# Two-layer hybrid decoder trunk: FFN parts of 4, 4 and 3 blocks, a first FFN block in one pass, and whole 512-column pieces

## The chip, the cores and the metric

The kernel runs on one core of one Trainium2 chip. The metric is the device time of one execution in microseconds (us), the median of the runs.

## The reference

The input x has 256 tokens of 2048 float32 values. Each of two layers computes, in float32:

```
h = RMSNorm(x);  x = x + mixer(h)            # mLSTM, forgetting attention, gated DeltaNet; ends in y @ w_out
h = RMSNorm(x);  x = x + (silu(h @ w_gate) * (h @ w_up)) @ w_down      # w_gate, w_up: 2048 x 5632
```

A last RMSNorm follows. The change touches the product with w_out at the end of the mixer, the whole FFN, and the norms' sums of squares.

## The kernel before

**Weights.** They lie in HBM in the order of use as units of 128 x 1024 float32 (512 KB). `unit` loads one into a `raw` buffer (3 buffers, SP's queue) and splits it: ScalarE writes the rounded `whi` (L140), VectorE the rest `wlo` (L141); there are 4 buffers of each. Activations are split into hi and lo in the same way. Each product is three matmuls, hi·whi, hi·wlo and lo·whi, into one PSUM bank. `block_b` does that for two token tiles of 128 (t = 0, 1), a weight piece of w columns and kts tiles of the contraction.

**PSUM.** There are eight banks: four of tag `d` (`dps`), two of `mg`, one each of `m0` and `m1` (`mps`).

**Order.** Tile's scheduler puts the instructions into the engines' queues. It follows the program's order but may take a later instruction ahead of one that is not ready by its own simulated times; each engine then runs its queue strictly in order. `tc.issue_after` holds instructions behind a given one. Semaphores come from the tiles.

**wo and the next norm.** The mixer's output product (L780 to 803) writes 512 columns of x at a time, the last 512 as two halves of 256. After each piece, `add_x` adds it into `xall` (VectorE), and `Norm.piece` transposes those columns (tile xT, by TensorE), splits them into the next operand `hs`, and sums squares. `Norm.scale` turns the sums into rstd (a power, by POOL) and into `rb`, rstd along the free axis, by two small matmuls (rbp) and a copy.

**FFN.** `ffn` (L810) takes the 5632 hidden columns in 11 blocks of 512, and the blocks in parts (`FF_PARTS`, 2, 2, 2, 2, 2, 1). After a part's blocks, its share of the product with w_down (`dn`) is added to x, in pieces of 512 columns; in the last part the last 512 come as two halves.

- The first block (`slow`) multiplies the unnormalised `hs`: all 16 k-tiles for gate (pg), then all 16 for up (pu). rstd is applied afterwards. Then `normalise(rb)` rescales `hs` in place for the other blocks, per k-tile: POOL adds hi and lo (yn, L841), VectorE multiplies by rb (L842), ScalarE rounds (L843), VectorE subtracts (L844); POOL forms the difference of the two token tiles (dt, L856; three sums st for the pairs), ScalarE and VectorE split that into `sd` (L829, L830).
- The other ten blocks (`fast`) use a 7-product scheme on two pairs of k-tiles (`quad`, k = 3 and 11) and a four-product form elsewhere (`plain`), in seven PSUM accumulators. Products 1, 6 and 7 end at k = 11 and are taken into `xs`, `ys`; products 2 to 5 end with the block, and VectorE and ScalarE form `ga`.
- Then the block's `ga` is transposed (tile hT, 8 transposes in two groups, bank `m0`) and split into `hid`, down's operand.

**The end.** In layer 1 the last half piece of down runs one token tile after the other (`block_b_halves`), and `Final.last` scales and stores each.

Of the kernel before, what the change touches and what calls it, by code (L numbers as in the profile page):

```python
# [23 lines left out]
KT = D // P  # L24
DFF = 5632
FT = DFF // P
FF_PARTS = (2, 2, 2, 2, 2, 1)
PAIRS = (3, 11)
HM, HF, HG = 4, 8, 4
EPS = 1e-6  # L30
# [29 lines left out]
def tile_trunk(ctx: ExitStack, tc: tile.TileContext, x: bass.AP, wu: bass.AP, prm: bass.AP,  # L60
# [170 lines left out]
        pool.tensor_tensor(out=r, in0=r, in1=mhalf[:, :cols], op=ALU.pow)  # L231
        return r

    PIECES = (slice(0, 512), slice(512, 1024), slice(1024, 1536), slice(1536, 1792), slice(1792, 2048))

    def square_sum(ssq, j, both=False):
        c = PIECES[j]
        w = c.stop - c.start
        for t in range(2):
            if both and t:  # L240
                junk = sp.tile([P, 512], BF16, tag="junkv", name="junkv", bufs=1)
                dve.scalar_tensor_tensor(out=junk[:, :w], in0=xall[:, t, c], scalar=1.0, in1=xall[:, t, c],
                                         op0=MUL, op1=MUL, accum_out=ssq[:, t, j:j + 1])
            else:
                junk = sp.tile([P, 512], BF16, tag="junk", name="junk", bufs=1)
                act.activation(out=junk[:, :w], in_=xall[:, t, c], func=AF.Square, accum_out=ssq[:, t, j:j + 1])
# [6 lines left out]
    class Norm:  # L253


        def __init__(self, l, off):
            self.l, self.off, self.hs = l, off, []
            self.ssq = small("ssq", [2, 5])

        def pair(self, k):  # L260
            ps = mps("xT")
# [8 lines left out]
                self.hs.append((hl[:, :S], hl[:, S:], hl))  # L270

        def piece(self, j):
            for k in range(PIECES[j].start // P, PIECES[j].stop // P, 2):
                self.pair(k)
            square_sum(self.ssq, j)

        def scale(self, first=False):
            if first:
                for j in range(5):
# [74 lines left out]
    def mixer(l, norm, nxt):  # L354
# [435 lines left out]
        for n in range(2):  # L790
            wout(n, groups[n], late, False, True)
            add_x(n, groups[n])
            nxt.piece(n)
        pst = [dps("wo") for t in range(2)]
        wout(2, pst, early + late, True, True)
        add_x(2, pst)
        nxt.piece(2)
        for c in range(2):
            pst = [dps("wo") for t in range(2)]
            for i, k in enumerate((0, 12, 4, 8)):  # L800
                block_b(l, "out", 1536 + c * S, pst, ys[k:k + 4], k, 4, i == 0, i == 3, S)
            add_x(3, pst, c * S, S)
            nxt.piece(3 + c)

    def add_x(n, pst, c=0, w=512, ts=(0, 1)):
        for t in ts:
# [3 lines left out]
    def ffn(l, norm, nxt):  # L810
# [19 lines left out]
            dve.tensor_tensor(out=e[:, 1], in0=v, in1=f32(e[:, 0]), op=SUB)  # L830
            return e[:, 0], e[:, 1]

        def normalise(rb):

            free = [sd[i][:, j] for i in range(5) for j in range(4)]
            free = [v.rearrange("p (h x) -> p h x", h=2) if len(v.shape) == 2 else v for v in free]
            y = [None, None]
            for k in range(KT):
                hi, lo, hl = hs[k]
                y[k % 2] = yk = sp.tile([P, S], F32, tag="ac", name="yn", bufs=2)  # L840
                pool.tensor_tensor(out=yk, in0=f32(hi), in1=f32(lo), op=ADD)  # L841
                dve.tensor_tensor(out=yk, in0=yk, in1=rb, op=MUL)  # L842
                act.activation(out=hi, in_=yk, func=AF.Copy)  # L843
                dve.tensor_tensor(out=lo, in0=yk, in1=f32(hi), op=SUB)  # L844
                if k - 1 in PAIRS:
                    y0 = y[1 - k % 2]
                    st = sp.tile([P, 384], F32, tag="pt", name="st", bufs=2)
                    s1, s2, s4 = (st[:, i * P:(i + 1) * P] for i in range(3))
                    pool.tensor_tensor(out=s1, in0=y0[:, P:], in1=yk[:, P:], op=ADD)
                    pool.tensor_tensor(out=s2, in0=s1, in1=y0[:, :P], op=SUB)  # L850
                    pool.tensor_tensor(out=s4, in0=yk[:, :P], in1=s2, op=SUB)
                    for n, v in (("s1", s1), ("s2", s2), ("s4", s4)):
                        ops[n, k - 1] = hilo(free.pop(), v)
                else:
                    v = sp.tile([P, S], F32, tag="tz", name="dt", bufs=2)[:, :P]
                    pool.tensor_tensor(out=v, in0=yk[:, :P], in1=yk[:, P:], op=SUB)  # L856
                    ops["d", k] = hilo(free.pop(), v)

        def quad(c, k):

# [31 lines left out]

        def fast(c, first):

            ps = {3: dps("p3")}
            for i in ((1, 6, 7) if first else (2, 4, 5)):
                ps[i] = dps(f"p{i}")
            for i, tag in zip((2, 4, 5) if first else (6, 7, 1), ("mg", "mg", "m1")):
                ps[i] = mps(f"p{i}", tag)
            seen = set()  # L900
            for k in range(KT):
                if k - 1 in PAIRS:
                    continue
                for i, (ahi, alo), (whi, wlo) in quad(c, k) if k in PAIRS else plain(c, k):
                    end = k == KT - 1 or (i in (1, 6, 7) and k == PAIRS[-1])
                    pe.matmul(ps[i], ahi, whi, start=i not in seen, stop=False)
                    pe.matmul(ps[i], ahi, wlo, start=False, stop=False)
                    pe.matmul(ps[i], alo, whi, start=False, stop=end)
                    seen.add(i)
                if k == PAIRS[-1]:  # L910
                    act.copy(out=xs[:, 0], in_=ps[1])
                    dve.tensor_tensor(out=xs[:, 1], in0=ps[6], in1=xs[:, 0], op=ADD)
                    dve.tensor_tensor(out=ys[:, 0], in0=ps[7], in1=xs[:, 1], op=ADD)
            for t, i, v in ((0, 2, xs[:, 0]), (1, 4, ys[:, 0])):
                dve.tensor_tensor(out=ga[:, t], in0=ps[i], in1=v, op=ADD)
                act.activation(out=ga[:, t], in_=ga[:, t], func=AF.Silu)
            dve.tensor_tensor(out=ys[:, 1], in0=ps[5], in1=xs[:, 1], op=ADD)
            dve.tensor_tensor(out=ys[:, 0], in0=ps[5], in1=ys[:, 0], op=ADD)
            dve.tensor_tensor(out=ys[:, 1], in0=ps[3], in1=ys[:, 1], op=ADD)
            for t in range(2):  # L920
                dve.tensor_tensor(out=ga[:, t], in0=ga[:, t], in1=ys[:, 1 - t], op=MUL)

        def slow(c):
            pg = [dps("pg") for t in range(2)]
            block_b(l, "gate", c, pg, hs, 0, KT, True, True)
            rstd, rb = norm.scale()
            for t in range(2):
                act.activation(out=ga[:, t], in_=pg[t], func=AF.Silu, scale=rstd[:, t:t + 1])
            pu = [dps("pu") for t in range(2)]
            block_b(l, "up", c, pu, hs, 0, KT, True, True)  # L930
            for t in range(2):
                dve.scalar_tensor_tensor(out=ga[:, t], in0=pu[t], scalar=rstd[:, t:t + 1], in1=ga[:, t],
                                         op0=MUL, op1=MUL)
            normalise(rb)

        for part, blocks in enumerate(FF_PARTS):
            nf = 4 * blocks
            fs = []
            for c in range(f0 * P, (f0 + nf) * P, 512):
                if c == 0:  # L940
                    slow(c)
                else:
                    fast(c, c == 512 or c == f0 * P)
                for q in range(0, 4, 2):
                    ps = mps("hT", "m0")
                    for i in range(2):
                        for t in range(2):
                            pe.transpose(ps[:, i * S + t * P:i * S + (t + 1) * P],
                                         ga[:, t, (q + i) * P:(q + i + 1) * P], ident)
                    hid = g4("hid", [2, 512], F32R, "gy")  # L950
                    act.copy(out=hid[:, 0], in_=ps)  # L951
                    dve.tensor_tensor(out=hid[:, 1], in0=ps, in1=f32(hid[:, 0]), op=SUB)
                    fs += [(hid[:, 0, i * S:(i + 1) * S], hid[:, 1, i * S:(i + 1) * S]) for i in range(2)]
            end = part == len(FF_PARTS) - 1
            for n in range(3 if end else 4):
                pst = [dps("dn") for t in range(2)]
                block_b(l, "down", n * 512, pst, fs, f0, nf, True, True)
                add_x(n, pst)
                if end:
                    nxt.piece(n)  # L960
            if end:
                for c in range(2):
                    pst = [dps("dn") for t in range(2)]
                    if c and l == depth - 1:
                        block_b_halves(l, "down", 1536 + c * S, pst, fs, f0, nf, S)
                        for t in range(2):
                            add_x(3, pst, c * S, S, (t,))
# [90 lines left out]
```

## Time and profile before

| | |
|---|---|
| median of 3 runs | 2416.74 us (2416.14 to 2416.99) |
| profiled execution | 2416.53 us, span 2414.6 us |
| TensorE busy | 2368.0 us, 98% of the span |
| VectorE, ScalarE, POOL busy | 1680.2, 1212.0, 278.3 us |
| mean granted TensorE clock | 0.992 |
| DMA | 435.89 MB, mean 181 GB/s |

Times are from the span's start. A stretch is read by its count of matmuls and the pace of one, since busy time of TensorE has modelled ends. Layer 0's FFN is 467.3 to 1209.6 us, layer 1's 1662.7 to 2405.

### The profile page before, as it was taken

To read this page: it belongs to the slowest core of one execution; us is meant where nothing else is said; L and a number is where in the kernel's file an instruction comes from. 1 tells how busy PE (TensorE), PEld (TensorE's weight loads), DVE (VectorE), ACT (ScalarE), POOL (GpSimd) and SP (SyncE) were. 2 spreads that over 40 slices of the span, in tenths; PEclk is the share of its full clock that TensorE was granted. 3 is DMA by queue.
4 is the path that set the end of the run, shared out by engine and by line. 5 is a ranking of instruction groups with operands and counts; after the bars stand their busy time and mean duration, and the time that the engine had idled before them with its cause. 6 is when DMAs were issued, how large, how long until landed. Compare 5 with 4: busy or idle time off the path is not lost.

```text
span 2414.6 us, 31866 instructions
## 1 busy us (share of the span) xinstructions
PE 2368.0 (98%) x11852; PEld 1995.4 (83%) x11852; DVE 1680.2 (70%) x2366; ACT 1212.0 (50%) x1783; POOL 278.3 (12%) x259
## 2 busy tenths in 40 slices
PE   9999999989999999999899999999999999999997
PEld 8888888867888888888798888888788888888886
DVE  5898655587676768576668976555866767676756
ACT  6754555554444444454466545555544444444443
POOL 0220000050101111010003000000501010111100
PEclk9999999999999999999999999999999999999998
DMA  6555455546565656665455554455465656565663
GB/s 218 167 174 175 138 166 176 176 166 198 175 210 191 200 185 200 191 198 183 151 169 175 175 163 152 155 186 192 148 200 191 201 169 213 192 196 186 203 203 114
DMA packets 120876, 435.89 MB, mean 181 GB/s; under 512 B 13584, under 2 KB 14480, under 8 KB 120720
## 3 DMA queue, kind: packets, MB, share of 16 engines
q1 hardware_dynamic: 120160, 432.70, 55.3%
q8 instruction: 93, 1.52, 0.3%
q10 hardware_dynamic: 560, 1.15, 0.1%
q14 instruction: 63, 0.52, 0.1%
HBM read 431.70 MB, written 2.10 MB: 180 GB/s over the span
## 4 chain that ended last, share of the span: by engine, by line
PE 88%; DVE 4%; issue 2%; ACT 2%; DMA 2%; POOL 1%; POOLq 0%; DVEq 0%; SPq 0%; ACTq 0%
PE p L70 31%; PE dn L70 19%; PE wo L70 7%; PE fq L70 4%; PE fk L70 4%; PE fv L70 4%; PE gkq L70 3%; PE mv L70 2%; DMA raw<-wu 2%; PE mq L70 2%; PE mk L70 2%; PE gvp L70 2%; PE gz L70 2%; PE pg L70 2%; DVE wlo L141 1%
## 5 line engine op out<-in xcount | busy, mean ns | idle before, releaser
L141 DVE TENSOR_TENSOR wlo<-raw,whi 128x1024 fp32r<-128x1024 f32 (+3 forms) x741 | 918.7, 1247 | 473.5 <-ACT whi L140 455.0
L140 ACT ACTIVATE whi<-raw 128x1024 fp32r<-128x1024 f32 (+3 forms) x741 | 775.8, 1053 | 772.2 <-PE dn L70 244.3
L70 PE MATMUL p<-whi,hl 128*128 128x512 f32 x1600 | 546.6, 391 | 1.0 <-ACT whi L140 1.0
L70 PE MATMUL dn<-whi,hid 128*128 128x512 f32 (+1 forms) x1440 | 444.3, 389 | 3.8 <-ACT hid L951 1.3
L70 PEld LDWEIGHTS p<-whi,hl 128*128 128x128 f32 x1600 | 301.3, 188 | 63.5 <-ACT whi L140 1.9
L70 PE MATMUL p<-wlo,hl 128*128 128x512 f32 x800 | 313.2, 392 | 7.1 <-DVE wlo L141 7.1
L70 PEld LDWEIGHTS dn<-whi,hid 128*128 128x128 f32 x1440 | 268.2, 189 | 60.0 <-ACT whi L140 3.0
L70 PE MATMUL dn<-wlo,hid 128*128 128x512 f32 (+1 forms) x720 | 277.2, 389 | 1.3 <-DVE wlo L141 1.3
L70 PE MATMUL p<-whi,sd 128*128 128x512 f32 x560 | 216.3, 391 | 0.0
L70 PEld LDWEIGHTS p<-wlo,hl 128*128 128x128 f32 x800 | 150.5, 188 | 41.0 <-DVE wlo L141 9.8
L874 POOL TENSOR_TENSOR rq<-rq 128x512 f32<-128x512 f32 x40 | 57.4, 1436 | 989.5 <-DVE rq L873 973.7
L70 PE MATMUL wo<-whi,yhl 128*128 128x512 f32 (+1 forms) x640 | 169.5, 351 | 0.0
L70 PEld LDWEIGHTS dn<-wlo,hid 128*128 128x128 f32 x720 | 136.5, 190 | 32.1 <-DVE wlo L141 5.2
L70 PEld LDWEIGHTS wo<-whi,yhl 128*128 128x128 f32 x640 | 112.6, 189 | 14.7
L70 PEld LDWEIGHTS p<-whi,sd 128*128 128x128 f32 x560 | 105.9, 189 | 21.6
L70 PE MATMUL wo<-wlo,yhl 128*128 128x512 f32 (+1 forms) x320 | 111.8, 349 | 0.0
L70 PE MATMUL p<-wlo,sd 128*128 128x512 f32 x280 | 109.8, 392 | 0.0
L878 ACT ACTIVATE th<-rq 128x1024 fp32r<-128x1024 f32 x80 | 84.0, 1050 | 43.8 <-POOL rq L876 27.8
L879 DVE TENSOR_TENSOR tl<-rq,th 128x1024 fp32r<-128x1024 f32 x80 | 99.8, 1248 | 3.5 <-ACT th L878 3.1
L876 POOL TENSOR_TENSOR rq<-rq 128x512 f32<-128x512 f32 x40 | 83.1, 2078 | 120.5 <-DVE rq L875 117.4
L871 DVE TENSOR_TENSOR wlo<-rq,whi 128x1024 fp32r<-128x1024 f32 x40 | 56.1, 1401 | 52.9 <-ACT whi L870 52.8
L870 ACT ACTIVATE whi<-rq 128x1024 fp32r<-128x1024 f32 x40 | 42.4, 1060 | 98.0 <-PE p L70 98.0
(362 smaller groups left out, 3527.2 us busy)
## 6 DMA issues: line engine op xcount, KB each, us to landing
raw<-wu SPq DMA_DIRECT2D x728, 512.0 KB, 4.2
rq<-wu SPq DMA_DIRECT2D x80, 512.0 KB, 4.2
raw<-wu SPq DMA_DIRECT2D x10, 420.0 KB, 3.0
xall<-x SPq DMA_DIRECT2D x3, 512.0 KB, 8.3
fw<-fnw SPq DMA_DIRECT2D x2, 512.0 KB, 6.8
out<-xall ACTq DMA_DIRECT2D x2, 512.0 KB, 3.3
out<-xall SPq DMA_DIRECT2D x2, 512.0 KB, 3.3
xall<-x SPq DMA_DIRECT2D x2, 256.0 KB, 4.4
```

Source lines behind the costliest of these rows:

```text
L70: self.log.append(nc.tensor.matmul(*a, **k).ins)
L140: act.activation(out=whi[:, c], in_=raw[:, c], func=AF.Copy)
L141: dve.tensor_tensor(out=wlo[:, c], in0=raw[:, c], in1=f32(whi[:, c]), op=SUB)
L870: act.activation(out=w1[0], in_=r1, func=AF.Copy)
L871: dve.tensor_tensor(out=w1[1], in0=r1, in1=f32(w1[0]), op=SUB)
L874: pool.tensor_tensor(out=b12, in0=b22, in1=b12, op=SUB)
L876: pool.tensor_tensor(out=b21, in0=b21, in1=b22, op=SUB)
L878: act.activation(out=hi, in_=v, func=AF.Copy)
L879: dve.tensor_tensor(out=lo, in0=v, in1=f32(hi), op=SUB)
```

## The change

The first block reads gate and up columns of one k-tile in one unit, has four accumulators open, and normalises a k-tile behind its matmuls. The transposes of a block's `ga` are kept as `pending` and issued inside the next `fast` block behind k = 5 and k = 7, or inside down's first piece behind its first two groups of four k-tiles. The parts are 4, 4 and 3 blocks. Which products of a block lie in the `d` banks now follows from its distance to the part's end. The last 512 columns of wo, and of down except at the end of layer 1, are one piece; the norms sum squares over four pieces.

```diff
-FF_PARTS = (2, 2, 2, 2, 2, 1)
+FF_PARTS = (4, 4, 3)
...
-    PIECES = (slice(0, 512), slice(512, 1024), slice(1024, 1536), slice(1536, 1792), slice(1792, 2048))
+    QUARTERS = tuple(slice(c, c + 512) for c in range(0, D, 512))
+    PIECES = QUARTERS[:3] + (slice(1536, 1792), slice(1792, 2048))
...
         def piece(self, j):
-            for k in range(PIECES[j].start // P, PIECES[j].stop // P, 2):
+            for k in range(4 * j, 4 * j + 4, 2):
                 self.pair(k)
             square_sum(self.ssq, j)
...
-        pst = [dps("wo") for t in range(2)]
-        wout(2, pst, early + late, True, True)
-        add_x(2, pst)
-        nxt.piece(2)
-        for c in range(2):
+        for n in range(2, 4):
             pst = [dps("wo") for t in range(2)]
-            for i, k in enumerate((0, 12, 4, 8)):
-                block_b(l, "out", 1536 + c * S, pst, ys[k:k + 4], k, 4, i == 0, i == 3, S)
-            add_x(3, pst, c * S, S)
-            nxt.piece(3 + c)
+            wout(n, pst, early + late, True, True)
+            add_x(n, pst)
+            nxt.piece(n)
...
-        def normalise(rb):
+        def normalise(k, rb):
...
-            ps = {3: dps("p3")}
-            for i in ((1, 6, 7) if first else (2, 4, 5)):
-                ps[i] = dps(f"p{i}")
+            ps = {i: dps(f"p{i}") for i in ((1, 6, 7, 3) if first else (2, 4, 5, 3))}
...
+                if k in (5, 7) and pending:
+                    hidden()
...
         def slow(c):
-            pg = [dps("pg") for t in range(2)]
-            block_b(l, "gate", c, pg, hs, 0, KT, True, True)
-            rstd, rb = norm.scale()
+
+            pg, pu = ([dps(n) for t in range(2)] for n in ("pg", "pu"))
+            for k in range(KT):
+                whi, wlo = unit(("s", l, "ug", c, k, 1, 1024))
+                for j, pst in ((1, pg), (0, pu)):
+                    w = slice(j * 512, (j + 1) * 512)
+                    for t in range(2):
+                        ahi, alo = half(k, t)
+                        pe.matmul(pst[t], ahi, whi[:, w], start=(k == 0), stop=False)
+                        pe.matmul(pst[t], ahi, wlo[:, w], start=False, stop=False)
+                        pe.matmul(pst[t], alo, whi[:, w], start=False, stop=(k == KT - 1))
+                if k == 0:
+                    rstd, rb = norm.scale()
+                normalise(k, rb)
...
-            pu = [dps("pu") for t in range(2)]
-            block_b(l, "up", c, pu, hs, 0, KT, True, True)
...
-            normalise(rb)
+
+        pending = []
+
+        def hidden():
+
+            fs, q = pending.pop(0)
+            ps = mps("hT", "m0")
+            with tc.issue_after(pe.log[-1]):
+                for i in range(2):
+                    for t in range(2):
+                        pe.transpose(ps[:, i * S + t * P:i * S + (t + 1) * P],
+                                     ga[:, t, (q + i) * P:(q + i + 1) * P], ident)
+            hid = g4("hid", [2, 512], F32R, "gy")
+            act.copy(out=hid[:, 0], in_=ps)
+            dve.tensor_tensor(out=hid[:, 1], in0=ps, in1=f32(hid[:, 0]), op=SUB)
+            fs += [(hid[:, 0, i * S:(i + 1) * S], hid[:, 1, i * S:(i + 1) * S]) for i in range(2)]
...
-                    fast(c, c == 512 or c == f0 * P)
...
+                    fast(c, (blocks - n) % 2 == 1)
+                pending += [(fs, 0), (fs, 2)]
             end = part == len(FF_PARTS) - 1
+            end = end and l == depth - 1
             for n in range(3 if end else 4):
                 pst = [dps("dn") for t in range(2)]
-                block_b(l, "down", n * 512, pst, fs, f0, nf, True, True)
+                for j in range(0, nf, 4):
+                    block_b(l, "down", n * 512, pst, fs[j:j + 4], f0 + j, 4, j == 0, j == nf - 4)
+                    if n == 0 and j < 8:
+                        hidden()
                 add_x(n, pst)
-                if end:
+                if part == len(FF_PARTS) - 1:
                     nxt.piece(n)
             if end:
                 for c in range(2):
                     pst = [dps("dn") for t in range(2)]
-                    if c and l == depth - 1:
+                    if c:
                         block_b_halves(l, "down", 1536 + c * S, pst, fs, f0, nf, S)
```

## Rows read from the trace of the kernel before

**Rows 1.** The page: busy time, share of the span and instructions of each engine.

```profile
PE 2368.0 (98%) x11852; PEld 1995.4 (83%) x11852; DVE 1680.2 (70%) x2366; ACT 1212.0 (50%) x1783; POOL 278.3 (12%) x259
```

**Rows 2.** The chain of waits, TensorE's pieces: start us, us, what, count.

```profile
447.26 10.80 PE wo L70 x90
...
472.39 0.33 PE xT L73 x3
...
1003.24 51.00 PE p L70 x225
```

**Rows 3.** Windows: stretch, us, then busy us (instructions) of each engine, granted clock, DMA.

```profile
467.30:1209.60 742.30, 727.05 (x3247) 596.69 (x3246) 520.47 (x572) 353.38 (x425) 100.11 (x77) 0.99 0.58 187
1662.70:2405.00 742.30, 727.54 (x3230) 596.31 (x3229) 520.06 (x573) 347.83 (x415) 100.99 (x75) 0.99 0.57 185
...
517.00:538.00 21.00, 14.41 (x54) 9.48 (x54) 19.95 (x30) 11.90 (x23) 15.57 (x15) 0.92 0.30 100
561.00:575.00 14.00, 12.82 (x57) 10.00 (x56) 11.62 (x14) 6.34 (x7) 0.00 (x0) 1.00 0.72 246
...
1174.00:1188.00 14.00, 7.49 (x27) 5.53 (x26) 8.06 (x11) 3.68 (x6) 0.00 (x0) 0.76 0.38 114
1712.50:1733.20 20.70, 15.15 (x54) 10.05 (x52) 19.65 (x30) 11.90 (x23) 15.56 (x15) 0.84 0.31 100
...
2370.00:2385.00 15.00, 8.49 (x28) 6.36 (x28) 8.48 (x12) 4.15 (x6) 0.00 (x0) 0.66 0.40 127
```

**Rows 4.** The same windows, instructions of tile xT alone.

```profile
467.30:1209.60 742.30, 3.15 (x20) 2.44 (x20) 4.15 (x9) 4.09 (x9) 0.99 0.58 187
1662.70:2405.00 742.30, 0.76 (x4) 0.52 (x4) 0.96 (x2) 0.93 (x2) 0.99 0.57 185
```

**Rows 5.** Timeline of TensorE at the last FFN part of layer 0.

```profile
1175.29 0.39 PE L70 MATMUL p<-whi,sd 128*128 128x512 f32 x1
1181.52 1.09 PE L73 MATMUL hT<-ident,ga 128*128 128x128 f32 x4 [5.84 <-DVE ga L921]
```

**Rows 6.** Timeline of VectorE in the same stretch.

```profile
1178.35 1.22 DVE L141 TENSOR_TENSOR wlo<-raw,whi 128x1024 fp32r<-128x1024 f32 x1
```

**Rows 7.** Timeline of TensorE in the block after the first.

```profile
528.01 0.65 PE L70 MATMUL p<-wlo,hl 128*128 128x512 f32 x1 [2.92 <-DVE wlo L141]
```

**Rows 8.** Groups by line, 489 to 545 us: busy us, mean ns | idle.

```profile
L141 DVE TENSOR_TENSOR wlo<-raw,whi 128x1024 fp32r<-128x1024 f32 x13 | 17.3, 1333 | 5.3 <-ACT whi L140 5.3
...
L856 POOL TENSOR_TENSOR dt<-yn 128x128 f32<-128x128 f32 x14 | 13.7, 980 | 30.8 <-DVE yn L842 28.5 <-ACT whi L870 1.4 <-ACT sd L829 0.9
L140 ACT ACTIVATE whi<-raw 128x1024 fp32r<-128x1024 f32 x13 | 13.6, 1048 | 1.6 <-PE p L70 1.5
...
L841 POOL TENSOR_TENSOR yn<-hl 128x256 f32<-128x256 f32 x14 | 12.0, 869 | 5.1 <-DVE hl L844 5.1
L842 DVE TENSOR_TENSOR yn<-yn,rb 128x256 f32<-128x256 f32 x16 | 9.7, 616 | 1.1 <-POOL yn L841 1.1
...
L830 DVE TENSOR_TENSOR sd<-dt,sd 128x128 fp32r<-128x128 f32 x14 | 7.4, 543 | 0.1
L844 DVE TENSOR_TENSOR hl<-yn,hl 128x256 fp32r<-128x256 f32 x16 | 7.3, 463 | 0.5 <-ACT hl L843 0.5
```

**Rows 9.** Two lines over the whole span: ns least/median/greatest, first and last start.

```profile
L842 DVE TENSOR_TENSOR yn<-yn,rb x32: 410/416/1489, 493.8 to 1737.2; 128x256 f32<-128x256 f32 x32
...
L830 DVE TENSOR_TENSOR sd<-dt,sd x28: 277/528/830, 496.9 to 1738.5; 128x128 fp32r<-128x128 f32 x28
```

**Rows 10.** Timelines of TensorE and POOL where the first FFN block begins.

```profile
467.32 0.40 PE L70 MATMUL pg<-whi,hl 128*128 128x512 f32 x1
...
470.19 0.71 POOL L231 TENSOR_TENSOR rstd<-rstd,mhalf 128x2 f32<-128x2 f32 x1 [45.94 <-DVE rstd L230]
```

**Rows 11.** The end: the chain of waits, and VectorE's timeline.

```profile
2406.32 1.38 issue
...
2407.51 0.15 DVE L230 TENSOR_SCALAR frstd<-fs 128x1 f32<-128x1 f32 x1
```

More of the change, by code (lines that the diff above doesn't have):

```diff
@@ L232, in rstd_of @@
         return r
-    PIECES = (slice(0, 512), slice(512, 1024), slice(1024, 1536), slice(1536, 1792), slice(1792, 2048))
+    QUARTERS = tuple(slice(c, c + 512) for c in range(0, D, 512))
+    PIECES = QUARTERS[:3] + (slice(1536, 1792), slice(1792, 2048))
     def square_sum(ssq, j, both=False):
-        c = PIECES[j]
+        c = (QUARTERS if ssq.shape[-1] == 4 else PIECES)[j]
         w = c.stop - c.start
@@ L257, in __init__ @@
             self.l, self.off, self.hs = l, off, []
-            self.ssq = small("ssq", [2, 5])
+            self.ssq = small("ssq", [2, 4])
         def pair(self, k):
@@ L278, in scale @@
             if first:
-                for j in range(5):
+                for j in range(4):
                     square_sum(self.ssq, j, True)
@@ L831, in hilo @@
             return e[:, 0], e[:, 1]
-        def normalise(rb):
[L835 to L857, printed above, removed]
@@ new lines, in ffn @@
+        free = [sd[i][:, j] for i in range(5) for j in range(4)]
+        yn = [None, None]
+        def normalise(k, rb):
+            hi, lo, hl = hs[k]
+            yn[k % 2] = yk = sp.tile([P, S], F32, tag="ac", name="yn", bufs=2)
+            pool.tensor_tensor(out=yk, in0=f32(hi), in1=f32(lo), op=ADD)
+            dve.tensor_tensor(out=yk, in0=yk, in1=rb, op=MUL)
+            act.activation(out=hi, in_=yk, func=AF.Copy)
+            dve.tensor_tensor(out=lo, in0=yk, in1=f32(hi), op=SUB)
+            if k - 1 in PAIRS:
+                y0 = yn[1 - k % 2]
+                st = sp.tile([P, 384], F32, tag="pt", name="st", bufs=2)
+                s1, s2, s4 = (st[:, i * P:(i + 1) * P] for i in range(3))
+                pool.tensor_tensor(out=s1, in0=y0[:, P:], in1=yk[:, P:], op=ADD)
+                pool.tensor_tensor(out=s2, in0=s1, in1=y0[:, :P], op=SUB)
+                pool.tensor_tensor(out=s4, in0=yk[:, :P], in1=s2, op=SUB)
+                for n, v in (("s1", s1), ("s2", s2), ("s4", s4)):
+                    ops[n, k - 1] = hilo(free.pop(), v)
+            else:
+                v = sp.tile([P, S], F32, tag="tz", name="dt", bufs=2)[:, :P]
+                pool.tensor_tensor(out=v, in0=yk[:, :P], in1=yk[:, P:], op=SUB)
+                ops["d", k] = hilo(free.pop(), v)
@@ L938, in ffn @@
             fs = []
-            for c in range(f0 * P, (f0 + nf) * P, 512):
+            for n in range(blocks):
+                c = (f0 + 4 * n) * P
                 if c == 0:
@@ L942, in ffn @@
                 else:
-                    fast(c, c == 512 or c == f0 * P)
[L944 to L953, printed above, removed]
+                    fast(c, (blocks - n) % 2 == 1)
+                pending += [(fs, 0), (fs, 2)]
             end = part == len(FF_PARTS) - 1
+            end = end and l == depth - 1
             for n in range(3 if end else 4):
                 pst = [dps("dn") for t in range(2)]
-                block_b(l, "down", n * 512, pst, fs, f0, nf, True, True)
+                for j in range(0, nf, 4):
+                    block_b(l, "down", n * 512, pst, fs[j:j + 4], f0 + j, 4, j == 0, j == nf - 4)
+                    if n == 0 and j < 8:
+                        hidden()
                 add_x(n, pst)
-                if end:
+                if part == len(FF_PARTS) - 1:
                     nxt.piece(n)
```

## The prediction

> **What bounds the kernel now.** I read the page's engine line first: TensorE alone is near its span [rows 1]. That share is made of modelled matmul ends, so it does not say whether TensorE keeps its pace. The pace comes from the chain of waits: 225 matmuls of 512 columns in 51.00 us are 0.227 us each, 90 of 256 columns in 10.80 us are 0.120, three transposes in 0.33 us are 0.11 [rows 2]. Below, "loss" is TensorE's elapsed time less its instructions at these paces.
>
> The windows over the two FFN stages come next: 742.3 us each [rows 3]. By the code, one holds 3084 matmuls of 512 columns (192 of the first block, ten blocks of 186, 1032 of down), 48 of 256 columns, 88 transposes hT (8 for each of 11 blocks) and 4 for rbp; xT adds 20 transposes in layer 0 and 4 in layer 1 [rows 4]. Layer 0: 3084 x 0.227 + 48 x 0.12 + 112 x 0.11 = 700.1 + 5.8 + 12.3 = 718.2, a loss of 24.1 us. Layer 1, with 96 transposes: 716.4, a loss of 25.9. Together 50.0 us. Narrow windows show where it sits [rows 3]:
> - After the first block, 54 instructions, 8 of them transposes, in 21.0 us need 46 x 0.227 + 8 x 0.11 = 11.3: loss 9.7. Layer 1: 20.7 less 11.3 is 9.4.
> - At the last FFN part, a single block, 27 instructions with 8 transposes in 14.0 us need 5.2: loss 8.8. Layer 1: 28 in 15.0 need 5.4, loss 9.6.
> - The other 50.0 - 37.5 = 12.5 us lie at the five part ends of each layer where a block of `fast` is followed by down, 1.25 each. The window from 561 shows one: 57 instructions, three of them transposes, need 12.6 of its 14.0 us.
>
> The timelines name the causes. In the last part nothing can stand between the block and its own down. The block's last matmul starts at 1175.29, the transposes at 1181.52, after 5.84 us of idle time that VectorE's ga ended [rows 5], and the granted clock of that window is 0.76 in place of 1.00 [rows 3]. The ga chain is long because weight splits (wlo, 1.22 us each) stand among its steps in VectorE's queue [rows 6]. After the first block TensorE waits for wlo, 2.92 us at the worst place [rows 7]: normalising 16 k-tiles falls on the up pass of 96 x 0.227 = 21.8 us, and VectorE falls behind.
>
> **The change, part by part.**
>
> *Parts of 4, 4, 3; transposes inside the next block or inside down.* No part is one block any more. A block's hT transposes come behind the next block's k = 5 and 7, or, for a part's last block, behind the first and second group of four k-tiles of down's first piece. A group is 24 matmuls, 5.4 us; the wait to be covered is the 6.2 us between the two starts above [rows 5]. Down does not need the late block's tiles until two groups (part of 3) or three (parts of 4) have run, 10.9 or 16.3 us. So the wait is covered if the queue holds the second group ahead of the transposes, and costs 6.2 - 5.4 = 0.8 us if it does not; with no cover at all it would cost what the single block costs now. The rule (blocks - n) % 2 ends each part in the form whose products 1, 6, 7 hold the banks that down takes next; those are evacuated after k = 12, so down's first matmul waits for no ga. There are 3 part ends per layer in place of 6. I take 0.4 us each, 2.4 in all: half of the uncovered 0.8 (bounds: 0, and today's 1.25 each, 7.5). Gain: 18.4 + 12.5 - 2.4 = 28.5 us. The transposes and down's matmuls are as many as before; 24 pieces of add_x go, on VectorE beside matmuls that cover them, so they are worth 0.
>
> *First block in one pass.* The 192 matmuls stay, 43.6 us; the DMAs stay 16 of 512 KB, one per 2.72 us, in the same order on SP's queue; each unit is split once as before. What moves is normalise: it begins when rb exists instead of 21.8 us in, and has up to 43.6 us of matmuls beside it. rb needs the row sums. Today rstd is ready at 470.90, 3.6 us after the first pg matmul [rows 10]; with the last piece of wo 512 wide its add_x and squares are longer, then come rbp and a copy, so I put rb at 5 to 7 us, while k = 2 runs. The rbp matmuls stand in TensorE's queue with the matmuls of the next k behind them, and those wait if rstd is late: 0 to 1 us.
>
> VectorE's need per k-tile, where normalise runs, is wlo 1.33 + yn 0.62 + hl 0.46 + sd 0.54 x 20/16 = 3.09 us [rows 8], against TensorE's 12 x 0.227 = 2.72. Over 16 k-tiles that makes VectorE 5.9 us late. The four whi/wlo buffers let the splits run three units ahead, 8.2 us less 1.05 + 1.23 for the split itself, so about 5.9 us of lateness is free. The same sum for the order of before (two k-tiles per unit, 1.33 + 2 x 1.76 = 4.85 us) gives 8 x 2.13 = 17.0 late, less 5.9 is 11.1, near the 9.7 that the window shows; for the new order it gives 0. Without disturbance the need is 1.22 + 0.41 + 0.46 + 0.28 x 20/16 = 2.4 us [rows 6, 8, 9]. But VectorE cannot begin until rb, so up to 5 us more may come late. The loss is between 0 and today's 9.7 per layer; I take 1.5, nearer the end that the sum gives. What spills over meets the next block, whose plain k-tiles leave VectorE 2.72 - 1.33 = 1.4 us each. Gain: 19.1 - 3.0 = 16.1 us.
>
> The stretched rows have one pattern: yn spreads from 0.41 to 1.49 us and sd from 0.28 to 0.83, while POOL works beside them [rows 8, 9]. The Trainium skill (SBUF — State Buffer, section Who interferes with whom) says that a VectorE instruction with two SBUF inputs contends with a GpSimd instruction that reads SBUF. That speaks against this edit, since the same POOL work moves under the gate half of the block, where the wlo splits run without it today. At the rule's worst the sum would be the first rival's; with no contention it would be 3 us under mine.
>
> *Pieces of 512 columns.* wo, per layer: 192 x 0.120 - 96 x 0.227 = 1.25 us less. down of layer 0: 48 x 0.120 - 24 x 0.227 = 0.3 less. down of layer 1 keeps halves, over 12 k-tiles in place of 4: 96 more halves for 48 wholes, 0.6 us more. Net 2.2 less. That k = 12 to 15 of the next operand arrive later costs nothing: they are needed 32 us into the first FFN block, or 16 us into mv of layer 1, and ready matmuls cover it.
>
> *The end.* The last two row halves become 36 matmuls, 4.3 us each, where they were 12, 1.4 us. Today the second half's frstd stands behind the first half's scaling in VectorE's queue, and the chain waits 1.38 us there [rows 11]. The first half will be done by then: 1.4 us less (0 to 2).
>
> *Small edits.* Four squares in place of five for the first norm, and sums over 4 columns: beside the loads at the start and matmuls elsewhere, 0.
>
> **Sum.** 28.5 + 16.1 + 2.2 + 1.4 = 48.2 us. The profiled execution took 2416.53 us, 2414.6 of it the span; the median of the runs is 2416.74. 2416.7 - 48.2 = 2368.5.
>
> **The rivals.**
> - *The first block stays bound by VectorE*, 9.7 us per layer as now. For: the stretched rows [rows 8, 9]. Against: twice the time, and the free lateness. 2368.5 + 16.1 = 2384.6 us.
> - *Small waits stay at the part ends*, for hT or hid, at today's price: 6 x (1.25 - 0.4) = 5.1. For: one group of down is shorter than the wait. 2373.6 us.
> - *Slower than before*: in the first block VectorE's queue follows one k-tile at a time, so that it stands still while POOL makes yn and dt, and the next wlo comes behind: 0.87 + 0.62 + 0.46 + 0.98 + 0.54 + 1.33 = 4.8 us per k-tile without ScalarE's steps [rows 8]. The rest of the change, with 3.0 left for this block and its 16.1, gives 51.2 us, 25.6 per layer, 1.6 per k-tile: this decides from 2.72 + 1.6 = 4.3 us. At 4.8 the time is 2416.7 + 2 x (16 x 2.08 - 25.6) = 2432 us. Against: in the order of before other k-tiles and wlo filled those gaps, as the check on 9.7 shows.
> - *It changes nothing*: the loss moves from part ends into the blocks. Against: 37.5 us are idle or slow time at four places that go. 2416 us.
>
> **How the numbers follow.** The forecast, with a loss in the first blocks under 4 us each, 0.60, and the second rival, 0.18, fill 2362 to 2377. First rival 0.13, slower 0.04, nothing or little 0.05, half of that within 0.2%. With every bound at its best the time is 2416.7 - 50.0 - 2.2 - 2 = 2362.5. The range, 2362 to 2385, leaves out the last two cases and little else. A measurement of this kernel tells 0.2%, 4.8 us, from no change: faster 0.93, same 0.03, slower 0.04.
>
> **What would show it.** No idle time of 5 us before hT and no FFN window with a granted clock of 0.76; yn beginning 5 to 7 us into the first block; at most 3 us of loss per FFN stage; no frstd behind the scaling at the end. The forecast is wrong if the first block takes over 48 us, if a wait of several us stands before dn or hT at a part end, or if layer 1's mixer, whose instructions are the same, takes another order and loses time there.

## The result and the profile after

The changed kernel takes 2374.82 us (median of 4 runs, 2373.77 to 2375.14) where the one before takes 2416.86 (4 runs, 2416.14 to 2418.01): 0.9825 of its time, 95% interval 0.9808 to 0.9842. That is 42.0 us less; 48.2 were forecast, 2368.5 us in a range of 2362 to 2385. The profiled execution took 2373.77 us, 42.8 less than that of before.

The page's engine line answers to [rows 1]:

```profile
PE 2351.0 (99%) x11684; PEld 1983.6 (84%) x11684; DVE 1662.5 (70%) x2310; ACT 1211.0 (51%) x1769; POOL 288.3 (12%) x259
```

No engine's work changed by more than 18 us; what went is time between TensorE's instructions. The windows answer to [rows 3]: the two FFN stages, the first block of layer 0, the stretch behind the first block in either layer, and a part end:

```profile
464.75:1190.40 725.65, 721.38 (x3233) 594.81 (x3232) 516.56 (x553) 356.65 (x428) 104.70 (x77) 1.00 0.57 192
1641.00:2364.30 723.30, 720.20 (x3281) 597.21 (x3279) 513.08 (x555) 350.66 (x419) 107.14 (x76) 1.00 0.57 190
464.75:509.69 44.94, 44.94 (x205) 37.26 (x204) 37.17 (x58) 25.22 (x48) 20.71 (x26) 1.00 0.51 165
509.69:527.53 17.84, 13.56 (x54) 9.51 (x53) 17.37 (x28) 12.89 (x22) 10.59 (x12) 1.00 0.46 157
1685.82:1703.67 17.85, 14.75 (x55) 10.75 (x54) 17.37 (x28) 12.89 (x22) 10.60 (x12) 0.90 0.46 160
640.00:665.00 25.00, 25.00 (x115) 20.70 (x115) 19.40 (x22) 12.72 (x14) 0.00 (x0) 1.00 0.73 246
```

Read with the paces of [rows 2] (0.227, 0.120 and 0.11 us). A window also counts an instruction that began before it and runs into it; the narrow stretches are therefore read by the instructions that start in them:

- By the code, layer 0's stage now has 3108 matmuls of 512 columns, and 32 xT, 88 hT and 4 rbp, which need 705.5 + 13.6 = 719.1 us of 725.7: loss 6.5, where it was 24.1. Layer 1's has 3036 whole ones, 144 of 256 columns and 100 of 128 columns, 717.5 of 723.3: loss 5.9, where it was 25.9. The two losses are 37.6 us smaller together.
- The first block has 192 matmuls, 8 transposes and 4 small matmuls rbp: 43.6 + 1.3 = 44.9 of 44.9 us. Nothing is lost inside it.
- Behind it, 53 matmuls start in either layer and need 12.0 us of 17.8: 5.8 us are lost in each. So 11.6 of the 12.4 us that are left lie in these two places.
- At a part end, 114 instructions, 8 of them transposes, need 24.9 of 25.0 us: nothing is lost. All six part ends share in the 0.8 us that are left elsewhere.

TensorE's timeline at that part end shows what stands in place of the 5.84 us before hT [rows 5]: the transposes come between matmuls of down, and no wait is named.

```profile
645.06 0.39 PE L70 MATMUL dn<-whi,hid 128*128 128x512 f32 x1
...
656.39 0.62 PE L70 MATMUL dn<-whi,hid 128*128 128x512 f32 x2
656.85 0.60 PE L73 MATMUL hT<-ident,ga 128*128 128x128 f32 x4
657.20 0.48 PE L70 MATMUL dn<-wlo,hid 128*128 128x512 f32 x1
...
662.75 0.60 PE L73 MATMUL hT<-ident,ga 128*128 128x128 f32 x4
```

The first transposes stand 52 matmuls behind down's first one, so the queue holds the second group ahead of them, and the 6.2 us of the ga chain are covered by 11.8.

Behind the first block, TensorE's timeline of layer 0 answers to [rows 7]. The waits are in brackets:

```profile
508.11 0.39 PE L70 MATMUL pg<-whi,hl 128*128 128x512 f32 x1
...
510.27 0.50 PE L70 MATMUL p<-wlo,hl 128*128 128x512 f32 x1 [0.19 <-DVE wlo L141]
...
513.15 0.50 PE L70 MATMUL p<-wlo,hl 128*128 128x512 f32 x1 [0.52 <-DVE wlo L141]
...
514.18 0.40 PE L70 MATMUL p<-whi,hl 128*128 128x512 f32 x1
516.76 0.50 PE L70 MATMUL p<-whi,sd 128*128 128x512 f32 x1 [2.18 <-ACT ga L934]
...
524.66 0.50 PE L70 MATMUL p<-wlo,hl 128*128 128x512 f32 x1 [1.30 <-DVE wlo L866]
```

Two kinds of wait stand here. The one at 516.76 is for ScalarE's silu of the first block: the product's PSUM bank still holds pg. The others are for weight splits of VectorE. ScalarE's timeline shows why silu is late: the normalise copies (L825) and a split stand ahead of it, then the load of its table.

```profile
510.56 0.31 ACT L825 ACTIVATE sd<-dt 128x128 fp32r<-128x128 f32 x1 [1.03 <-POOL dt L851]
...
513.45 0.31 ACT L825 ACTIVATE sd<-st 128x128 fp32r<-128x128 f32 x1 [0.92 <-POOL st L846]
513.66 1.04 ACT L140 ACTIVATE whi<-raw 128x1024 fp32r<-128x1024 f32 x1
514.72 1.28 ACT L934 ACT_TABLE_LOAD   x1
516.02 0.69 ACT L934 ACTIVATE ga<-pg,rstd 128x512 f32<-128x512 f32 x1
```

The last matmul of pg starts at 508.11, so that silu's input is there some 7 us before silu runs. ScalarE sits idle for POOL in between, 1.03 and 0.92 us, with silu further back in its queue.

In layer 1 the same wait for the bank is followed by matmuls 0.43 us apart, the pace of the 1.2 GHz level (the granted clock of that window is 0.90, and 0.50 from 1693.51 to 1696.07), and the later wait shrinks from 1.30 to 0.15 us:

```profile
1692.92 0.80 PE L70 MATMUL p<-whi,sd 128*128 128x512 f32 x1 [2.18 <-ACT ga L934]
1693.51 0.63 PE L70 MATMUL p<-wlo,sd 128*128 128x512 f32 x1
1693.94 0.63 PE L70 MATMUL p<-whi,sd 128*128 128x512 f32 x1
...
1700.81 0.50 PE L70 MATMUL p<-wlo,hl 128*128 128x512 f32 x1 [0.15 <-DVE wlo L866]
```

The slow matmuls there cost about what the later wait costs in layer 0 (5.8 us in all in either layer). That VectorE catches up while TensorE is slow fits the shorter wait and is not shown otherwise.

When normalise begins is read from TensorE's, ScalarE's and VectorE's timelines in the first block; rstd, which was at 470.19 [rows 10], now starts on POOL at 467.85:

```profile
478.61 0.61 PE L70 MATMUL rbp<-ident,rstd 128*128 128x128 f32 x4
```

```profile
479.25 0.37 ACT L287 COPY rb<-rbp 128x256 f32<-128x256 f32 x1 [0.92 <-PE rbp L70]
```

```profile
479.73 0.76 DVE L837 TENSOR_TENSOR yn<-yn,rb 128x256 f32<-128x256 f32 x2
...
519.94 0.41 DVE L837 TENSOR_TENSOR yn<-yn,rb 128x256 f32<-128x256 f32 x1
```

rstd is done at 468.56, but rbp uses the bank of xT and comes ten us behind it: the first yn is 15.0 us into the block. The sixteenth starts at 519.94, 40.2 us later for 15 steps, 2.68 us per k-tile, and 10.2 us into the next block.

At the end, VectorE's timeline answers to [rows 11]: the second half's frstd follows its sum directly, 0.7 us behind the end of the last add_x; the first half's scaling was over at 2363.3.

```profile
2362.86 0.41 DVE L323 TENSOR_SCALAR xall<-xall,frstd 128x384 f32<-128x384 f32 x1
2364.39 0.42 DVE L804 TENSOR_TENSOR xall<-dn,xall 128x256 f32<-128x256 f32 x1 [1.12 <-PE dn L70]
...
2365.51 0.15 DVE L230 TENSOR_SCALAR frstd<-fs 128x1 f32<-128x1 f32 x1
```

In elapsed time the two FFN stages are 35.7 us shorter, less than their losses, since they now hold 2 us more work at these paces, most of it sixteen transposes xT (1.8 us) that fell outside before. The span is 42.6 us shorter (2372.0 for 2414.6), so 7.0 us of it lie outside the stages: the first FFN block starts 2.6 us earlier (464.75 for 467.32), layer 1's mixer with its piece of wo is 2.5 us shorter, and the end 1.9.

### The profile page after: what moved, and what is told of

It is laid out like the page before. It is cut to its first block, busy times and chain, and to the rows that moved or that the text cites. A ratio compares the mean times of both kernels' runs of the same rounds, so it can differ in the third digit from the quotient of the medians.

```text
span 2372.0 us, 31449 instructions
## 1 busy us (share of the span) xinstructions
PE 2351.0 (99%) x11684; PEld 1983.6 (84%) x11684; DVE 1662.5 (70%) x2310; ACT 1211.0 (51%) x1769; POOL 288.3 (12%) x259
## 4 chain that ended last, share of the span: by engine, by line
PE 94%; DVE 3%; ACT 1%; POOL 1%; issue 1%; DMA 1%; POOLq 0%; SPq 0%; DVEq 0%; ACTq 0%
PE p L70 35%; PE dn L70 20%; PE wo L70 7%; PE fq L70 4%; PE fk L70 4%; PE fv L70 4%; PE gkq L70 3%; PE mv L70 2%; PE mq L70 2%; PE mk L70 2%; PE gvp L70 2%; PE gz L70 2%; DVE wlo L141 1%; PE hT L73 1%; ACT whi L140 1%; PE fs L70 1%
## 5 line engine op out<-in xcount | busy, mean ns | idle before, releaser
L70 PE MATMUL dn<-whi,hid 128*128 128x512 f32 (+1 forms) x1456 | 437.8, 383 | 0.0
L869 POOL TENSOR_TENSOR rq<-rq 128x512 f32<-128x512 f32 x40 | 68.5, 1713 | 911.9 <-DVE rq L868 911.9
L70 PE MATMUL wo<-whi,yhl 128*128 128x512 f32 x512 | 161.5, 393 | 0.0
L874 DVE TENSOR_TENSOR tl<-rq,th 128x1024 fp32r<-128x1024 f32 x80 | 111.6, 1395 | 20.3 <-ACT th L873 19.2
L70 PEld LDWEIGHTS wo<-whi,yhl 128*128 128x128 f32 x512 | 96.0, 188 | 19.5
L70 PE MATMUL wo<-wlo,yhl 128*128 128x512 f32 x256 | 100.6, 393 | 0.0
L871 POOL TENSOR_TENSOR rq<-rq 128x512 f32<-128x512 f32 x40 | 84.3, 2107 | 112.1 <-DVE rq L870 99.6
L70 PE MATMUL p<-th,sd 128*128 128x512 f32 x240 | 89.0, 390 | 0.0
L70 PE MATMUL fv<-whi,hl 128*128 128x512 f32 x256 | 82.8, 397 | 0.0
```

The source lines that it names most:

```text
L70: self.log.append(nc.tensor.matmul(*a, **k).ins)
L869: pool.tensor_tensor(out=b12, in0=b22, in1=b12, op=SUB)
L871: pool.tensor_tensor(out=b21, in0=b21, in1=b22, op=SUB)
L874: dve.tensor_tensor(out=lo, in0=v, in1=f32(hi), op=SUB)
```

## The experiments

Each is an edit of the changed kernel. "Loss" is that of the two FFN stages in the profiled execution, as above (starts of TensorE's instructions against the paces). Ratios are to the kernel before on the same chip; their intervals are some 0.0015 to either side, 3.6 us, so small differences are read from the losses; but a loss is that of one run (f1's profiled run took 1.7 us more than the median of its runs).

| run | median us | ratio, 95% interval | loss, layers 0 and 1, us |
|---|---|---|---|
| changed kernel | 2374.82 | 0.9825 [0.9808, 0.9842] | 6.5, 5.9 |
| e1_two_pass | 2381.04 | 0.9857 [0.9841, 0.9874] | 9.7, 10.6 |
| e2_old_parts | 2402.55 | 0.9946 [0.9931, 0.9961] | 19.1, 20.3 |
| e3_inline | 2376.01 | 0.9835 [0.982, 0.9849] | 6.7, 6.9 |
| e4_own_bank | 2377.63 | 0.984 [0.9826, 0.9855] | 8.2, 7.8 |
| f1_early_table | 2377.67 | 0.9841 [0.9828, 0.9855] | 9.5, 8.4 |
| f2_no_pool_add | 2372.13 | 0.9817 [0.9804, 0.9831] | 5.8, 6.7 |
| f3_defer | 2378.63 | 0.9844 [0.983, 0.9857] | 8.3, 7.1 |
| f4_halves | 2377.74 | 0.9842 [0.9828, 0.9855] | 7.1, 6.7 |
| g1_spread | 2375.41 | 0.9826 [0.9813, 0.984] | 7.1, 6.4 |
| g2_spread_early | 2374.47 | 0.9824 [0.9811, 0.9838] | 7.0, 6.2 |
| g3_no_low | 2381.47 | 0.9853 [0.984, 0.9867] | 8.8, 10.4 |
| g4_no_low_early | 2376.14 | 0.9831 [0.9818, 0.9845] | 7.3, 7.5 |

### What each part of the change is worth

**e1_two_pass:** the first block in two passes again, normalise behind them; the lines are the code as it then stands.

```
             pg = [dps("pg") for t in range(2)]
             block_b(l, "gate", c, pg, hs, 0, KT, True, True)
             rstd, rb = norm.scale()
...
             block_b(l, "up", c, pu, hs, 0, KT, True, True)
...
             for k in range(KT):
                 normalise(k, rb)
```

> The changed kernel with the first FFN block in two passes again, all else changed. In the changed kernel TensorE loses 5.7 us behind the first block of each layer, with two passes it lost 9.9 there. If the one pass is worth the difference, this takes 2374.8 + 2 x 4.2 = 2383 us, and the trace shows 9 to 10 us of loss after the first block. Rival: the one pass gives nothing, since normalise starts late in it anyway; then 2374 to 2377 us.

2381.04 us, 6.2 more; the losses rise by 3.2 and 4.7 us, 7.9 in all. One pass brings 6 to 8 us, where 16.1 were forecast.

**e2_old_parts:** parts of 2, 2, 2, 2, 2, 1; the transposes wait only where down needs them.

```
-FF_PARTS = (4, 4, 3)
+FF_PARTS = (2, 2, 2, 2, 2, 1)
...
+                    while len(fs) < j + 4:
+                        hidden()
...
-                    if n == 0 and j < 8:
+                    if pending:
                         hidden()
```

> The changed kernel with the parts 2, 2, 2, 2, 2, 1 again; a part's waiting transposes are issued before the group of down that needs them. If the part sizes are what took the losses away, the single last block is back with 8.8 to 9.6 us per layer, and the part ends with their small losses (1.25 each at most): 2374.8 + 18.4 + 0 to 12 = 2393 to 2405 us. Rival: moving the transposes is what helps, whatever the parts; then 2375 to 2380 us.

2402.55 us, 27.7 over the changed kernel; the losses rise by 27.0. TensorE's timeline has the idle time of the single block back:

```profile
1173.95 1.09 PE L73 MATMUL hT<-ident,ga 128*128 128x128 f32 x4 [5.83 <-DVE ga L916]
```

The part sizes carry two thirds of the gain.

**e3_inline:** parts of 4, 4, 3, but each block's transposes are written right behind it, with nothing that holds them.

```
-            with tc.issue_after(pe.log[-1]):
...
                 pending += [(fs, 0), (fs, 2)]
+                while pending:
+                    hidden()
...
```

> The changed kernel with each block's transposes issued right behind the block, as before the change, parts of 4, 4, 3 kept. If part sizes carry the gain and the queue already put the transposes among later matmuls, only the six part ends can lose, up to 1.25 us each: 2375 to 2382 us. Rival: the place of the transposes carries it, each part end then waits about 6 us for ga: 2374.8 + 36 = 2411 us.

2376.01 us, and 1.2 more lost: within what a measurement tells from no change. The queue sets late transposes behind later matmuls by itself; where the program writes them matters little once a block or down follows.

**f4_halves:** wo's last 512 columns as two halves again.

```
...
+        for c in range(2):
+            pst = [dps("wo") for t in range(2)]
+            for i, k in enumerate((0, 12, 4, 8)):
+                block_b(l, "out", 1536 + c * S, pst, ys[k:k + 4], k, 4, i == 0, i == 3, S)
+            add_x(3, pst, c * S, S)
+            nxt.half(c)
```

> The changed kernel with the last 512 columns of wo as two halves of 256 again, in both layers; all else changed. By the pace of halves (0.120 us against 0.227 / 2) it is 2 x 1.25 us slower: 2377.3 us. Rival: the halves bring the last k-tiles, the row sums and so rb earlier and normalise begins earlier, and that pays for them: 2373 to 2375 us.

2377.74 us, 2.9 more; 2 x 1.25 were expected from the paces. In its trace the stretches ahead of the two FFN stages are 1.6 us longer each, 0.4 of it four transposes xT that moved there, and the losses rise by 1.5 in all. The first yn comes 9.9 us into the block in place of 15.0, as the rival had it, but nothing is gained by that.

### What is left behind the first block

**e4_own_bank:** rbp in a bank of tag `mg`, so that it need not wait for xT.

```
-                    rstd, rb = norm.scale()
+                    rstd, rb = norm.scale(tag="mg")
```

> The changed kernel with rbp of the FFN norm in a bank of mg, which is free there, in place of the bank that the xT transposes use in turn. In the changed kernel rstd is ready at 468.6 us but rbp runs at 478.6, and yn begins at 479.7. If rb waits for the xT bank and the late start is what leaves 5.7 us of loss per layer, yn begins at 471 to 474 and the loss falls to 2 to 3.5 us: 2368 to 2371 us. Rival: the loss comes from the bank that the next block's third product takes over from pg, which waits for the silu on ScalarE (2.2 us of it), and from the pace of VectorE and POOL; then yn begins earlier and the time stays at 2374 to 2376 us.

VectorE's timeline has the first yn 5.4 us earlier:

```profile
474.31 0.75 DVE L837 TENSOR_TENSOR yn<-yn,rb 128x256 f32<-128x256 f32 x2
```

The last starts at 516.29, 3.7 us earlier; yet the losses rise to 8.2 and 7.8, and 2377.63 us is above both ranges. TensorE waits longer for a split, and for the bank as before:

```profile
514.54 0.50 PE L70 MATMUL p<-wlo,hl 128*128 128x512 f32 x1 [2.03 <-DVE wlo L141]
...
518.45 0.80 PE L70 MATMUL p<-whi,sd 128*128 128x512 f32 x1 [1.99 <-ACT ga L934]
```

My theory that the late rb makes the loss fell.

**f1_early_table:** a silu of one element beside rstd, so that its table is there.

```
                     rstd, rb = norm.scale()
+                    warm = small("tab", [1], 1)
+                    act.activation(out=warm, in_=rstd[:, 0:1], func=AF.Silu)
```

> The changed kernel with one more silu of a 128x1 operand behind rstd, so that ScalarE's table is loaded early in the first FFN block; the order of the queues is otherwise the same. In the changed kernel the next block's third product waits 2.35 us beyond its pace for a bank that the silu of pg must free, and the table load of 1.28 us stands right ahead of that silu. If the wait is for ScalarE's queue, it shrinks by 1.28 us in each layer: 2374.8 - 2.6 = 2372 us, and up to 1 us less where TensorE's clock does not fall. Rival: VectorE's lateness comes right behind it and takes the time back in later waits for wlo: 2374 to 2375 us.

2377.67 us, above both ranges. The wait for the bank falls from 2.18 to 0.75 us. The time comes back, and more, at the quad of k = 3:

```profile
515.48 0.50 PE L70 MATMUL p<-whi,sd 128*128 128x512 f32 x1 [0.75 <-ACT ga L936]
...
522.76 0.50 PE L70 MATMUL p<-whi,hl 128*128 128x512 f32 x1 [0.86 <-ACT whi L865]
524.80 0.80 PE L70 MATMUL p<-wlo,hl 128*128 128x512 f32 x1 [1.31 <-DVE wlo L866]
525.39 0.63 PE L70 MATMUL p<-whi,hl 128*128 128x512 f32 x1
```

**f2_no_pool_add:** normalise without POOL's sum of hi and lo.

```
-            pool.tensor_tensor(out=yk, in0=f32(hi), in1=f32(lo), op=ADD)
-            dve.tensor_tensor(out=yk, in0=yk, in1=rb, op=MUL)
+            dve.tensor_tensor(out=yk, in0=f32(hi), in1=rb, op=MUL)
```

> The changed kernel with POOL's addition of hi and lo left out of normalise: VectorE multiplies hi alone by rb, so the low parts do not enter the other ten blocks. POOL loses 16 instructions of 0.8 us per layer beside VectorE. If contention with POOL, and the steps that wait for POOL, make normalise late, VectorE's yn takes about 0.41 us, the last tiles are done near the block's end, and the loss of 5.7 us per layer falls to 0 to 2.4: 2363.5 to 2368 us. Rival: the loss is the silu behind its table load, and in-order queues of ScalarE: the wait of 2.35 us stays and only the waits for wlo go: 2369 to 2372 us.

2372.13 us, 2.7 less and at the edge of what the rival said, with a ratio 0.0008 lower, inside both intervals; the profiled losses, 5.8 and 6.7, are together those of the changed kernel (12.5 and 12.4). So a gain is not shown, though much changed inside. The groups by line of the two kernels, 479 to 531 us (busy us, mean ns | idle before); first the changed kernel, then this one:

```profile
L837 DVE TENSOR_TENSOR yn<-yn,rb 128x256 f32<-128x256 f32 x16 | 8.0, 513 | 0.8 <-POOL yn L836 0.6
L839 DVE TENSOR_TENSOR hl<-yn,hl 128x256 fp32r<-128x256 f32 x16 | 7.9, 506 | 0.0
L826 DVE TENSOR_TENSOR sd<-dt,sd 128x128 fp32r<-128x128 f32 x14 | 7.2, 531 | 0.0
```

```profile
L838 DVE TENSOR_TENSOR hl<-yn,hl 128x256 fp32r<-128x256 f32 x16 | 6.9, 449 | 0.0
L836 DVE TENSOR_TENSOR yn<-hl,rb 128x256 f32<-128x256 f32 x16 | 6.6, 433 | 0.1
L826 DVE TENSOR_TENSOR sd<-dt,sd 128x128 fp32r<-128x128 f32 x14 | 4.5, 324 | 2.6 <-ACT sd L825 2.3
```

The same VectorE steps are 5.1 us shorter without that POOL work beside them. The rule of the Trainium skill (SBUF — State Buffer, section Who interferes with whom), that VectorE's instructions with two SBUF inputs contend with GpSimd's reads, agrees with this. What those 5.1 us are worth in the kernel's time is not shown: 2.7 us by the medians, nothing by the losses. The next block starts at 509.00 here, and VectorE's timeline has the last yn right behind that:

```profile
509.84 0.43 DVE L836 TENSOR_TENSOR yn<-hl,rb 128x256 f32<-128x256 f32 x1
```

That is 0.8 us into the next block, in place of 10.2; the last subtraction (L838) still ends 8.2 us into it. The waits for wlo all but go (0.19 us in layer 0, 0.54 in layer 1). The wait for the bank stays, and matmuls 0.43 us apart follow it:

```profile
515.52 0.51 PE L70 MATMUL p<-whi,sd 128*128 128x512 f32 x1 [2.48 <-ACT ga L933]
...
516.68 0.63 PE L70 MATMUL p<-wlo,hl 128*128 128x512 f32 x1
```

**f3_defer:** k-tiles 10 to 15 are normalised in the next block, from its first k-tile, held behind the first silu.

```
...
-                normalise(k, rb)
+                if k < 10:
+                    normalise(k, rb)
...
+                if later:
+                    n, rb, silu = later.pop(0)
+                    with tc.issue_after(silu):
+                        normalise(n, rb)
...
```

> The changed kernel with normalise of k = 10 to 15 traced inside the next block, ScalarE's steps of it held behind the silu of pg. All work is kept. If what costs 5.7 us per layer is that the last k-tiles' steps stand in the in-order queues ahead of the silu and of the next block's weight splits, the loss falls to 0 to 2 us per layer: 2364 to 2368 us. Rival: VectorE simply has too much to do there, and the work moved into the next block is lost in that block: 2374 to 2376 us.

2378.63 us, above both ranges. The wait for the bank is gone, and one for the quad's split takes its place, with slow matmuls behind:

```profile
523.69 0.80 PE L70 MATMUL p<-wlo,hl 128*128 128x512 f32 x1 [3.46 <-DVE wlo L866]
524.29 0.63 PE L70 MATMUL p<-whi,hl 128*128 128x512 f32 x1
```

**g1_spread and g2_spread_early:** the same six k-tiles, each held behind VectorE's split of the next block's k-tiles 5 to 10; g2 has f1's early table as well.

```
...
+                if later and k >= 5:
+                    with tc.issue_after(unit.last.ins):
+                        normalise(*later.pop(0))
...
```

> The last six k-tiles (10 to 15) are normalised in the next block, each behind VectorE's split of the low weights of its k-tiles 5 to 10, so that neither the first block nor the quad of tiles 3 and 4 shares VectorE with them. Theory that VectorE has simply too much between 479 and 530 us (busy 28.1 of 30 us and 20.5 of 21 us there, against 53 of 70 us behind it): the loss behind the first block falls from 5.7 us to 0 to 3 us per layer, no wait for the low weights L866 is left, and the time is 2364 to 2370 us. Rival, that what is moved always comes back at its new place, as in the run that normalised them from the next block's start: a wait of 2 us or more at tiles 5 to 12 of the next block with matmuls 0.43 us apart behind it, 2373 to 2379 us.

> As the run that spreads tiles 10 to 15 over the next block, and ScalarE's table for silu is loaded beside rstd, before the first k-tile is normalised. Theory of VectorE's load: the wait for the bank that pg holds until silu (2.35 us) is gone as well, 0 to 1.5 us lost per layer, 2362 to 2367 us, 0 to 3 us under the run without the early table. Rival: the wait for the bank was already gone with ScalarE's shorter queue, then the same as that run within 1 us; or all of it comes back, 2373 to 2379 us.

2375.41 and 2374.47 us: the same as the changed kernel, the times of the rivals. The loss moved once more, and the early table bought nothing. TensorE's timeline of g1 has waits at the first quad, and again at the second, which needs the operands that were put off. They are shorter than the 2 us that the rival named, and no matmuls 0.43 us apart follow them:

```profile
522.12 0.73 PE L70 MATMUL p<-th,sd 128*128 128x512 f32 x2 [1.46 <-ACT th L873]
...
546.36 0.50 PE L70 MATMUL p<-wlo,hl 128*128 128x512 f32 x1 [1.20 <-DVE wlo L866]
```

**g3_no_low and g4_no_low_early:** VectorE's L839 left out; g4 with the early table.

```
-            dve.tensor_tensor(out=lo, in0=yk, in1=f32(hi), op=SUB)
```

> VectorE's subtraction L839 of normalise is left out (the low halves of the normalised hl stay those from before the scaling, in the other ten blocks too): sixteen VectorE steps of 0.41 to 1.3 us less per layer, some 8 to 9 us of the 48.7 us that it is busy between 479 and 530 us, nothing else. Theory of VectorE's load: the waits for the low weights behind the block are gone, the wait for pg's bank (2.35 us) stays since ScalarE's order is the same, 2 to 3.5 us lost per layer, 2367 to 2371 us. Rival, that the bank and the half clock behind it make the loss whatever VectorE has to do: 5 to 6 us lost per layer, 2373 to 2376 us.

> As the run without the subtraction L839 (the low halves of hl stay those from before the scaling), with the table for silu loaded early as well. Theory of VectorE's load: both waits gone, 0 to 2 us lost per layer, 2363 to 2367 us; with the table alone the time had gone up to 2377.7 us. Rival, that another engine's step (POOL's sums, ScalarE's copies) takes the place of VectorE: 4 us or more lost per layer, 2371 us or more.

2381.47 us is slower than either theory said, though VectorE has less to do; 2376.14 us, with 7.3 and 7.5 us lost, is what g4's rival said. VectorE's timeline of g3 shows what no sum of its work shows:

```profile
508.97 1.22 DVE L141 TENSOR_TENSOR wlo<-raw,whi 128x1024 fp32r<-128x1024 f32 x1
...
512.07 0.43 DVE L837 TENSOR_TENSOR yn<-yn,rb 128x256 f32<-128x256 f32 x1 [0.90 <-POOL yn L836]
512.41 1.22 DVE L141 TENSOR_TENSOR wlo<-raw,whi 128x1024 fp32r<-128x1024 f32 x1
514.32 0.29 DVE L826 TENSOR_TENSOR sd<-dt,sd 128x128 fp32r<-128x128 f32 x1 [0.69 <-ACT sd L825]
...
515.86 1.22 DVE L141 TENSOR_TENSOR wlo<-raw,whi 128x1024 fp32r<-128x1024 f32 x1
```

The queue's order changed with the edit: each split now stands behind a yn that waits for POOL and an sd that waits for ScalarE. The splits come every 3.45 us, where TensorE takes a unit every 2.72, though VectorE waits for 0.90 + 0.69 us of each round. This is the mechanism of the prediction's third rival, at 3.45 instead of 4.8 us, and for a few k-tiles only.

## Why the prediction came out as it did

**Part ends, parts and transposes: right, and a little too careful.** All six part ends lose nothing; 0.4 us each were left. e2 gives 27.7 us for the part sizes, e3 1.2 for the place of the transposes; 28.5 were forecast together. The queue did hold the second group ahead of hT.

**First block: the mis-sized term.** I left 1.5 us per layer; 5.8 are lost in each, 8.6 us more in both. That is more than the 5.4 us by which the two profiled executions' difference falls short of 48.2; the part ends (2.4 better) make up part of it. The direction was right: 9.7 and 9.4 before, by the prediction's windows. Those count an instruction that began before them, as above; by starts the 9.7, 9.4, 8.8 and 9.6 are 9.9, 9.8, 9.3 and 9.8, and 11.2 us in place of 12.5 are left for the other part ends. Three steps of the working failed:

- rb was put at 5 to 7 us into the block; the first yn came at 15.0. Some 5 us of that is rbp's wait for xT's bank: with a bank of its own (e4) the first yn comes at 9.8, still later than I put it. But e4 and f4 (9.9) lose no less than the changed kernel, so this alone does not set the loss.
- VectorE's need per k-tile was taken as 3.09 us; it went at 2.68, busy 38.7 of the 40.6 us from the first yn to the last, so that the pace was better than the sum had it. With the late start normalise still ran 10.2 us into the next block, up to its quad of k = 3. That the free lateness I counted on was used up by the late start is argued, not shown.
- The sum counted VectorE alone. It had no term for the PSUM bank that pg holds until ScalarE's silu, which stands in its queue behind normalise copies that wait for POOL (1.03 and 0.92 us) and a 1.28-us table load: 2.18 us of waiting, the largest single one.

What the experiments settle is that none of these waits, taken away alone, takes the loss away. The late rb (e4, f4), the table load (f1), six k-tiles at two other places (f3, g1) or VectorE's subtraction (g3), each gave its time back at another step of the ring POOL, VectorE, ScalarE, where each engine takes the next step of its queue or waits for it. Without POOL's sum (f2) the waits for VectorE all but went, and the bank, 2.48 us, with the half clock behind it took what that saved. That the loss goes only with two things at once, yn done by the block's end (nearly so in f2) and silu early (as in f1), is argued from these runs and not shown; that pair was not run. So the 11.6 us are located and what ends each wait is known, but what would remove them stays open.

**Pieces and the end: right.** f4 gives 2.9 us for wo's pieces where 2.5 were counted in a net 2.2; its trace, 3.9 us longer, has 2.4 for the pieces (2 x 1.6 less 2 x 0.4) and the rest in the FFN stages. No frstd stands behind the scaling any more, and the end is 1.9 us shorter where 1.4 were counted.

**Rivals.** VectorE did not bind the first block at 9.7 us per layer, but part of that rival came true: 5.8 us, between its 9.7 and my 1.5, though the largest wait in it is ScalarE's. No small waits stayed at the part ends. The forecast's own signs held but for yn's beginning and the 3 us per stage.

## What to carry to other kernels

Time that an engine idles because nothing independent follows a block is the surest gain: larger parts, so that other work always follows, brought 28 of the 42 us. Where several engines with in-order queues hand one tile round, a sum of each engine's work is only a lower bound (g3 took work from VectorE and was 6.7 us slower): add the hand-offs, ask what each queue holds in front of the step that frees a PSUM bank, and expect that a wait taken out alone may come back at another step, as it did here.

## What the runs showed of the hardware

The same wait had two prices. After 2.18 us for the bank, with waits of 0.19 and 0.52 us ahead of it in layer 0 and 0.21 and 0.55 in layer 1, TensorE kept 0.23 to 0.24 us per matmul in layer 0 (granted clock 1.00 from 517.10 to 519.40) and went at 0.43 us, the 1.2 GHz level, in layer 1 (0.50 from 1693.51 to 1696.07, six matmuls). What tells the two apart stays open.
